# A two-layer trunk on one core: feed-forward blocks in pairs, with one sum per pair

## The chip, the core and the metric

The kernel runs on one core of a Trainium2 chip. The core has TensorE for matrix products, VectorE and ScalarE for element-wise work, GpSimd, and SyncE, whose queue (SP) starts nearly all transfers here. Each engine works through its own list of instructions in order, and semaphores tie the lists together. TensorE writes its sums into accumulator memory (PSUM), of which the kernel uses eight banks of 128 x 512 float32. The metric is the device time of the whole program in microseconds, as the median of several runs.

## The reference

Input is x of 1024 positions with 1024 channels. Two layers follow, each a token mixer and then a feed-forward part, with a layer norm after every part:

```python
for i in range(DEPTH):                      # DEPTH = 2
    mix = rwkv7_time_mix(h, ...) if i % 2 == 0 else s5_mix(h, ...)
    h = layer_norm(DN_ALPHA * h + mix, ln_g[2 * i], ln_b[2 * i])
    h = layer_norm(DN_ALPHA * h + sq_relu_mlp(h, mlp_w1[i], mlp_w2[i]), ...)

def sq_relu_mlp(x, w1, w2):                 # w1: 1024 x 4096, w2: 4096 x 1024
    return jnp.square(jax.nn.relu(x @ w1)) @ w2
```

The change lies in `sq_relu_mlp`. It is the largest part: two layers of two products of 1024 x 1024 x 4096.

## The kernel before

**Layout and halves.** Activations lie with channels on the 128 partitions and positions along the columns. The 1024 positions are worked in two halves of 512, called A (`hA`, its operand `xo`) and B (`hB`, `xoB`), each in eight tiles of 128 x 512.

**Three products for one.** Every float32 operand is split into a rounded high part and a low part: ScalarE casts (`S.copy`, L191), VectorE subtracts (L192). A product of two tiles is then three matmuls (`mm3`: high x high, high x low, low x high). A weight tile is loaded by SP into `wraw` (two buffers) and split into `whi` and `wlo` (three buffers each). It serves 12 matmuls of 512 columns.

**Blocks.** The 4096 inner channels are cut into 16 blocks of 256 (`KB2` = 2 tiles of 128). In `blocks`, `up(b)` makes two sums of 24 matmuls each, and for each of them Relu (L1126) and Square (L1127) on ScalarE and the split into the buffer `qbuf`. `down(b)` takes these two operands, makes eight sums of 6 matmuls, and VectorE adds each to the state (L1158; L1156 for the first block). `mlp` runs layer 0 so: `up(0)`, then for each b `up(b + 1)` and after it `down(b)`. The sums take banks in turn from `psd()`, three of them in layer 0, seven in the feed-forward of layer 1.

**Layer 1.** The first JB = 3 blocks run plainly for A, and later the same three for B. The other 13 run jointly for both halves (`both`): a scheme with seven products of half the inner length in place of eight, 84 matmuls up, and 96 down. It needs sums and differences of the halves, split into operands T1 to T4 (`tops`); T1 lies in the place of `qbuf`, T4 in the place of A's operand. For the plain blocks the low parts of the weights are made beforehand: while layer 0 works on B, `presplit` loads 24 weight tiles, splits them and stores the low parts in memory (`low`), and the plain blocks of layer 1 load these in place of the subtraction on VectorE (L224 is their cast).

**What sets the order.** A scheduler places the instructions on each engine by priority (the program's order, unless `rank` sets a base) in a model of the time. So the order on each engine is fixed when the program is built. Work such as the norm of one half is cut into steps that are woven in: each `weave(op, share)` lets `share` steps follow a VectorE operation of the feed-forward (`PACEU` for the splits of `up`, `PACED` for the adds of `down`).

**Around it.** In layer 0 the feed-forward of A runs partly beside the recurrence of half B. After 12 blocks (`INS1`) the projection `wo(1)` of half B is placed, and the norm of B is woven into the last blocks. Then the tables of the S5 mixer, the norm of A and the S5 scan of A run beside the feed-forward of B. `INS3` is the number of blocks of B after which the mixer's output is loaded (`yload`).

Of the kernel before, what the change touches and what calls it, by code (L numbers as in the profile page):

```python
# [22 lines left out]
INS1 = 12  # L23
INS2 = 13
VSH = (-1, 2, 2, 4, 64)
INS3 = 12
# [9 lines left out]
PRE = 6  # L36
PACEU = (2.0, 7.0)
PACED = (0.5, 1.3)
PREB = 3
JB = 3  # L40
# [39 lines left out]
def trunk(ctx, tc, A):  # L80
# [127 lines left out]
    def wload(src, kt, n, key=None, halved=False):  # L208
# [3 lines left out]
        for k0 in range(0, kt, step):  # L212
# [12 lines left out]
            else:  # L225
                split(raw, hi, lo, G if nw[0] % WLG[0] in WLG[1] and WLG[2] <= nw[0] < WLG[3] else V)
                if key and key[0] not in ("mw1", "mw2"):
# [5 lines left out]
    def presplit(tiles):  # L233

        for key, k0, src in tiles:
            raw = tp.tile([128, 512], F32, tag="la", name="pre", bufs=2)
            SP.dma_start(raw, src.rearrange("p k n -> p (k n)"))
            hi = tp.tile([128, 512], F32R, tag="m", name="prehi", bufs=2)
            S.copy(hi, raw)
            behind(V.tensor_sub(raw.bitcast(F32R), raw, hi.bitcast(F32)))  # L240
            low[key, k0] = dr.tile([128, 512], F32, name=f"low{len(low)}")
            SP.dma_start(low[key, k0], raw)
            for _ in range(PRE):
                yield 1
# [869 lines left out]
    def blocks(i, h, xo, qbuf):  # L1114
# [4 lines left out]
        def up(b):  # L1119
            qs[b] = []  # L1120
            pace_[0] = PACEU[i]
            for n in range(KB2):
                p = psd()
                dense(p, wload(A["mw1"][i, b * KB2 + n], KT, 128, ("mw1", i, b * KB2 + n)), xo)
# [8 lines left out]
        def kept(src, part):  # L1133
# [4 lines left out]
            SP.dma_start(lo.bitcast(F32).rearrange("p k n -> p (k n)"), part)  # L1138
            S.copy(hi, raw)
            return [(hi[:, k], lo[:, k]) for k in range(KB2)]  # L1140

        def down(b, first=False, cs=slice(0, HT), keep=None):
            for n2 in range(C // nw):
                if keep is None:
                    w = wload(A["mw2"][i, b, n2], KB2, nw, ("mw2", i, b, n2))
                else:
                    if (b, n2) not in keep:
                        keep[b, n2] = kept(A["mw2"][i, b, n2], low[("mw2", i, b, n2), 0])
                    w = keep[b, n2]
                for n in range(nw // 128):  # L1150
                    p = psd()[:, cs]
                    dense(p, [(x[:, n * 128 : (n + 1) * 128], y[:, n * 128 : (n + 1) * 128]) for x, y in w],
                          [(x[:, cs], y[:, cs]) for x, y in qs[b]])
                    z = h[n2 * (nw // 128) + n][:, cs]
                    if first:
                        weave(V.scalar_tensor_tensor(z, z, ALPHA, p, op0=ALU.mult, op1=ALU.add), PACED[i])  # L1156
                    else:
                        weave(V.tensor_add(z, z, p), PACED[i])  # L1158

        return up, down  # L1160

    def mlp(i, h, xo, qbuf):

        nb = 32 // KB2
# [439 lines left out]
    for n in range(INS3):  # L1604
        next(mb)
        if n == PREB:
            first_steps(presplit([((("mw1", 1, b * KB2 + n), k0, A["mw1"][1, b * KB2 + n][:, k0 : k0 + 4]))
                                  for b in range(JB) for n in range(KB2) for k0 in (0, 4)]
                                 + [((("mw2", 1, b, n2), 0, A["mw2"][1, b, n2])) for b in range(JB) for n2 in range(C * KB2 // 512)]), 99000)
    ys = yload(0)  # L1610
    run(mb)
    unweave()
# [31 lines left out]
    def second_half():  # L1644
        yield from norm_steps(hB, 2, 1, True, xoB)
        for k in range(4):
            a = t3[k]
            G.tensor_add(a, a, hB[k])
# [3 lines left out]
            tops[1].append(d)  # L1652

# [3 lines left out]
    for b in range(JB - 1):  # L1657
        ua(b + 1)
        da(b, b == 0)
# [112 lines left out]
```

## Time and profile before

| What | Value |
|---|---|
| median of 3 runs | 2596.31 us (2596.01 to 2599.6) |
| the profiled execution, its own time | 2585.47 us |
| its span, first to last instruction | 2583.5 us |
| mean granted clock of TensorE | 0.975 |
| busy: TensorE, VectorE, ScalarE, GpSimd | 95%, 69%, 47%, 16% |
| matmuls | 16684 |

In the trace a line number is that of the kernel's text, and that of a helper where the helper issues the instruction: L256 is every dense matmul, L191 and L192 are every split. Buffer numbers are left out, so `d` is any bank of a dense sum. Matmuls are pipelined, and each row's length overlaps the next one's; what one matmul costs is read from the distance between starts.

The stages, in us from the start: the recurrence with little beside it up to about 775; the recurrence of B beside the feed-forward of A up to 1040; the projection, the norm of B, the last blocks of A and the tables up to 1295; the S5 scan of A up to 1400; the feed-forward of B up to 1640; S5 of B and the gated outputs up to 1877; plain blocks of A up to 1950; joint blocks up to 2470; plain blocks of B, the last norm and the stores up to the end.

### The profile page before, as it was taken

Reading aid. Unit: us, or ns where it says so; the run is one execution under the profiler, and the core shown is the slowest. Engines: PE = TensorE matmul, PEld = TensorE weight load, DVE = VectorE, ACT = ScalarE, POOL = GpSimd, SP = SyncE. Lnnn points to the kernel's source line nnn. Section 1 sums busy time; section 2 is a strip of 40 time slices with the busy share of each in tenths; the row PEclk is TensorE's granted clock in tenths of the full one; section 3 lists DMA queues with packets and bytes.
Section 4 is the critical chain, followed back from the end, with each engine's and each line's share of the span. In section 5 each row is a group of like instructions: output and inputs, shape, how many; then the busy total and the mean of one; then the engine's idle time right before and its main releaser. Section 6 shows DMA issues by size and latency. Waiting matters only on the chain.

```text
span 2583.5 us, 43873 instructions
## 1 busy us (share of the span) xinstructions
PE 2466.0 (95%) x16684; PEld 2002.0 (77%) x16684; DVE 1794.0 (69%) x3443; ACT 1210.5 (47%) x2165; POOL 406.0 (16%) x336
## 2 busy tenths in 40 slices
PE   7989989989989999999999999999999999999997
PEld 5779767788767888777777878887887888888886
DVE  7477687577787776899886665676657555656555
ACT  7555575454454443345634444334565333343334
POOL 3110441331211102001000000100222111111111
PEclk9999989999899999999999999999999999999998
DMA  4765455664222324446565553244261111111233
GB/s 152 261 200 184 160 198 172 190 186 152 93 70 78 104 86 126 141 122 165 162 226 192 176 175 111 95 162 160 94 197 60 49 54 50 48 58 49 78 122 114
DMA packets 217682, 340.66 MB, mean 132 GB/s; under 512 B 21248, under 2 KB 81792, under 8 KB 217472
## 3 DMA queue, kind: packets, MB, share of 16 engines
q1 hardware_dynamic: 216320, 335.77, 40.9%
q8 instruction: 131, 2.15, 0.4%
q10 hardware_dynamic: 1152, 2.10, 0.2%
q14 instruction: 79, 0.65, 0.1%
HBM read 267.53 MB, written 70.25 MB: 131 GB/s over the span
## 4 chain that ended last, share of the span: by engine, by line
PE 69%; DVE 13%; DMA 9%; ACT 5%; issue 3%; SPq 1%; POOL 0%; ACTq 0%; DVEq 0%; POOLq 0%
PE d L256 51%; PE d L1195 10%; DVE wlo L192 2%; PE pA L672 1%; DMA wraw<-in_mw_dram 1%; ACT whi L191 1%; DMA yl<-s_y 1%; DVE hA L1158 1%; DMA pre<-in_mw_dram 1%; DMA ldsg<-s_sg 1%; DMA s_y<-yg 1%; PE pR L780 1%; DMA lda<-s_a 1%; DVE oAl L192 1%; PE pq L934 1%
## 5 line engine op out<-in xcount | busy, mean ns | idle before, releaser
L191 ACT CAST whi<-wraw 128x512 fp32r<-128x512 f32 x424 | 261.6, 619 | 487.1 <-PE d L256 249.8
L192 DVE TENSOR_TENSOR wlo<-wraw,whi 128x512 fp32r<-128x512 f32 x424 | 317.4, 750 | 201.1 <-ACT whi L191 197.2
L256 PE MATMUL d<-qbuf,whi 128*128 128x512 f32 x1152 | 365.2, 399 | 9.8 <-ACT rl L1126 4.7
L256 PE MATMUL d<-oAh,whi 128*128 128x512 f32 (+1 forms) x752 | 303.2, 409 | 13.1 <-ACT ev L493 5.5
L256 PE MATMUL d<-oAl,whi 128*128 128x512 f32 (+1 forms) x752 | 302.1, 403 | 7.7 <-DVE oAl L942 4.4
L256 PE MATMUL d<-oAh,wlo 128*128 128x512 f32 (+1 forms) x752 | 301.2, 404 | 3.5 <-DMA wlo<-low 1.9
L256 PEld LDWEIGHTS d<-qbuf,whi 128*128 128x128 f32 x1152 | 212.2, 189 | 63.1 <-DVE hA L1158 7.8
L256 PE MATMUL d<-qbuf,wlo 128*128 128x512 f32 x576 | 225.5, 394 | 0.0
L256 PE MATMUL d<-oBh,whi 128*128 128x512 f32 x496 | 195.9, 395 | 0.4 <-DVE hA L1158 0.4
L256 PE MATMUL d<-oBh,wlo 128*128 128x512 f32 x496 | 195.8, 395 | 0.0
L256 PE MATMUL d<-oBl,whi 128*128 128x512 f32 x496 | 193.7, 391 | 0.0
L256 PEld LDWEIGHTS d<-oAh,whi 128*128 128x128 f32 (+1 forms) x752 | 143.1, 192 | 48.0 <-ACT ev L493 7.8
L256 PEld LDWEIGHTS d<-oAl,whi 128*128 128x128 f32 (+1 forms) x752 | 144.4, 193 | 38.7 <-DVE oAl L942 4.8
L256 PEld LDWEIGHTS d<-oAh,wlo 128*128 128x128 f32 (+1 forms) x752 | 144.3, 193 | 36.2 <-DVE wlo L192 2.7
L256 PE MATMUL d<-ql,whi 128*128 128x512 f32 x416 | 163.1, 392 | 0.0
L256 PE MATMUL d<-qh,whi 128*128 128x512 f32 x416 | 162.0, 389 | 0.0
L256 PE MATMUL d<-qh,wlo 128*128 128x512 f32 x416 | 158.0, 394 | 0.0
L256 PEld LDWEIGHTS d<-qbuf,wlo 128*128 128x128 f32 x576 | 108.9, 189 | 24.4 <-issue 0.5
L1158 DVE TENSOR_TENSOR hA<-hA,d 128x512 f32<-128x512 f32 x136 | 92.0, 683 | 28.8 <-PE d L256 27.7
L1158 DVE TENSOR_TENSOR hB<-hB,d 128x512 f32<-128x512 f32 (+1 forms) x160 | 97.6, 631 | 20.1 <-PE d L256 18.9
L256 PEld LDWEIGHTS d<-oBh,wlo 128*128 128x128 f32 x496 | 93.2, 188 | 21.9 <-issue 0.8
L256 PEld LDWEIGHTS d<-oBh,whi 128*128 128x128 f32 x496 | 93.3, 188 | 21.5 <-issue 2.0
(495 smaller groups left out, 5268.6 us busy)
## 6 DMA issues: line engine op xcount, KB each, us to landing
wraw<-in_mw_dram SPq DMA_DIRECT2D x356, 256.0 KB, 2.7
wlo<-low SPq DMA_DIRECT2D x92, 256.0 KB, 2.9
wraw<-in_glu_dram SPq DMA_DIRECT2D x64, 256.0 KB, 2.7
low<-wlo SPq DMA_DIRECT2D x52, 256.0 KB, 2.6
raw<-in_mw_dram SPq DMA_DIRECT2D x52, 256.0 KB, 2.7
wraw<-in_wk_dram SPq DMA_DIRECT2D x32, 256.0 KB, 3.2
wraw<-in_wr_dram SPq DMA_DIRECT2D x32, 256.0 KB, 3.7
wraw<-in_wv_dram SPq DMA_DIRECT2D x32, 256.0 KB, 4.2
```

Of the source, the lines that this page charges most:

```text
L191: S.copy(hi, src)
L192: op = (e or V).tensor_sub(lo, src, hi.bitcast(F32))
L256: bulk.append((PE.matmul(p, w, x, **kw).ins, x.shape[-1]))
L672: prods.append(PE.matmul(pp[h][:, cc, i], D.KB[j][hs, u].rearrange("p j l -> p (j l)"), D.AR[j][hs, u].rearrange("p j l -> p (j l)"), star ...
L780: hop.append(PE.matmul(pR[hs, i], at[:, h, c, i, 0], vsa[:, cl, h, i], start=True, stop=True))
L934: PE.matmul(pq[:, j : j + 1], q[:, j * 128 : (j + 1) * 128], ones_c[:, 0:1], start=k + j == 0, stop=k == KT - 1, skip_group_check=True)
L1158: weave(V.tensor_add(z, z, p), PACED[i])
L1195: PE.matmul(p, w[:, k], x, start=not add and k + j == 0, stop=k == 3 and j == 2, skip_group_check=True)
```

## The change

`mlp` and the plain blocks of layer 1 now work in pairs: `up(b)`, `up(b + 1)`, then one `down((b, b + 1))`. This takes two banks at a time and adds the products of both blocks in them, 12 matmuls per bank, so that VectorE adds to the state once per pair. For each two banks the order is: both banks with block b, then both with block b + 1; in the first two banks block b + 1 is taken one operand at a time. `INS1` and `INS3` count pairs now (6 = 12 blocks).

In layer 1 there are JB = 4 plain blocks per half, two pairs, and 12 joint ones. `presplit` and the stored low parts of feed-forward weights are gone: VectorE splits these weights where they are used. `PACEU` is 2.0 in both layers (7.0 before in layer 1), `PACED` 0.5 (1.3 before in layer 1). The operand T4 is made step by step in `second_half` together with T2, from a copy, and no longer between the last plain up phase and the joint blocks.

```diff
-INS1 = 12
+INS1 = 6
-INS3 = 12
+INS3 = 6
-PACEU = (2.0, 7.0)
-PACED = (0.5, 1.3)
-JB = 3
+JB = 4
...
-        def down(b, first=False, cs=slice(0, HT), keep=None):
+        def down(bs, first=False, cs=slice(0, HT), keep=None):
...
+                nn = nw // 128
+                ps = [psd()[:, cs] for _ in range(nn)]
+                parts = [(w[k], qs[b][k]) for w, b in zip(ws, bs) for k in range(KB2)]
+                def products(n, js):
+                    for j in js:
+                        (x, y), (qh, ql) = parts[j]
+                        sl = slice(n * 128, (n + 1) * 128)
+                        mm3(ps[n], x[:, sl], y[:, sl], qh[:, cs], ql[:, cs], j == 0, j == len(parts) - 1)
+                last = len(parts) - 1
+                groups = [range(KB2 * m, KB2 * m + KB2) for m in range(len(bs))]
+                if n2 == 0 and len(bs) > 1:
+                    groups[-1:] = [(j,) for j in groups[-1]]
+                turns_ = [(n, js) for js in groups for n in range(nn)]
...
-        up(0)
-        for b in range(nb):
-            if b + 1 < nb:
-                up(b + 1)
-            down(b, b == 0)
+        for b in range(0, 32 // KB2, 2):
+            up(b)
+            up(b + 1)
+            down((b, b + 1), b == 0)
             yield
...
-    for b in range(JB - 1):
-        ua(b + 1)
-        da(b, b == 0)
+    ua(1)
+    da((0, 1), True)
+    ua(2)
+    ua(3)
     unweave()
...
-    for b in range(JB - TB):
-        ub(b + 1)
-        db(b)
-    for b in range(JB - TB + 1, JB):
-        ub(b)
+    ub(1)
+    db((0, 1))
+    ub(2)
+    ub(3)
```

**TensorE, a down phase of half B in layer 0.** `d_16863` is the last sum of an up phase, `qbuf` the operands of the down phase, `whi` and `wlo` its weights. Before:

```order
L256 MATMUL d_16863<-oBh_12551,wlo_16873 128x512
L256 MATMUL d_16911<-qbuf_9633,whi_16907 128x512 x2
L256 MATMUL d_16911<-qbuf_9633,wlo_16908 128x512
...
L256 MATMUL d_16919<-qbuf_9633,whi_16907 128x512 x2
...
L256 MATMUL d_16933<-qbuf_9633,whi_16929 128x512 x2
L256 MATMUL d_16933<-qbuf_9633,wlo_16930 128x512
```

After the change, with `d_16471` as the last sum of the pair's up phases, `whi_16515` as block b's weights and `whi_16521` as those of block b + 1:

```order
L239 MATMUL d_16471<-oBh_12399,wlo_16481 128x512
L239 MATMUL d_16525<-qbuf_9633,whi_16515 128x512 x2
...
L239 MATMUL d_16526<-qbuf_9633,whi_16515 128x512 x2
...
L239 MATMUL d_16525<-qbuf_9633,whi_16521 128x512 x2
L239 MATMUL d_16525<-qbuf_9633,wlo_16522 128x512
L239 MATMUL d_16526<-qbuf_9633,whi_16521 128x512 x2
L239 MATMUL d_16526<-qbuf_9633,wlo_16522 128x512
L239 MATMUL d_16565<-qbuf_9633,whi_16555 128x512 x2
...
L239 MATMUL d_16525<-qbuf_9633,whi_16521 128x512
L239 MATMUL d_16526<-qbuf_9633,whi_16521 128x512
```

Before, each bank is closed after 6 matmuls, and the block that the up phase has just made is not read. Now two banks stay open, and the operand of the last up phase is first read in the last two rows: after 6 + 6 matmuls with block b, 3 + 3 with the first operand of block b + 1, and 6 of the next bank, which the scheduler has pulled forward.

**VectorE, the start of the joint blocks in layer 1.** `raw` and `s2` are the first joint weights, `oAl` is a part of T4, `t2` of T2, `t1r` goes into T1, the adds to `hA` are those of the last plain blocks. Before:

```order
L1158 TENSOR_TENSOR hA_7722<-hA_7722,d_20432 128x512
L192 TENSOR_TENSOR t2_20267<-t3r_19672,t2_20266 128x512
L1670 TENSOR_TENSOR t3r_19632<-t3r_19632,hB_12067 128x512
L192 TENSOR_TENSOR wlo_20484<-raw_20470,whi_20483 128x512
L1158 TENSOR_TENSOR hA_7762<-hA_7762,d_20440 128x512
L192 TENSOR_TENSOR t2_20280<-t3r_19686,t2_20279 128x512
L192 TENSOR_TENSOR wlo_20503<-s2_20479,whi_20502 128x512
L1158 TENSOR_TENSOR hA_7802<-hA_7802,d_20454 128x512
L192 TENSOR_TENSOR oAl_20364<-t3r_19618,oAh_20363 128x512
L1158 TENSOR_TENSOR hA_7842<-hA_7842,d_20462 128x512
L192 TENSOR_TENSOR wlo_20520<-raw_20472,whi_20519 128x512
L192 TENSOR_TENSOR qbuf_20349<-t1r_19616,qbuf_20349 128x512
```

After the change:

```order
L188 TENSOR_TENSOR oAl_20014<-tb_19977,oAh_20013 128x512
L1157 TENSOR_TENSOR hA_7682<-hA_7682,d_20083 128x512
L188 TENSOR_TENSOR wlo_20153<-wraw_20150,whi_20152 128x512
L188 TENSOR_TENSOR wlo_20159<-wraw_20156,whi_20158 128x512
L1157 TENSOR_TENSOR hA_7722<-hA_7722,d_20122 128x512
L1157 TENSOR_TENSOR hA_7762<-hA_7762,d_20123 128x512
L188 TENSOR_TENSOR wlo_20204<-raw_20190,whi_20203 128x512
L188 TENSOR_TENSOR wlo_20223<-s2_20199,whi_20222 128x512
L1157 TENSOR_TENSOR hA_7802<-hA_7802,d_20162 128x512
L1157 TENSOR_TENSOR hA_7842<-hA_7842,d_20163 128x512
L188 TENSOR_TENSOR wlo_20240<-raw_20192,whi_20239 128x512
L188 TENSOR_TENSOR qbuf_20017<-t1r_19184,qbuf_20017 128x512
```

T2 and T4 now stand before this place, the first among the weights of the plain blocks, and the splits of those weights (`wraw`) have come in.

**SP, the feed-forward of half B in layer 0.** `wraw` are weights of the running blocks, `pre` and `low` the loads and stores of `presplit`. Before:

```order
L242 DMA low64_15918<-pre_15913 128x512
L215 DMA wraw_16022<-in_mw1_dram 128x512
L237 DMA pre_16028<-in_mw2_dram 128x512
L215 DMA wraw_16065<-in_mw1_dram 128x512
L242 DMA low65_15991<-pre_15986 128x512
L215 DMA wraw_16071<-in_mw1_dram 128x512
L242 DMA low66_16033<-pre_16028 128x512
L237 DMA pre_16077<-in_mw2_dram 128x512
```

After the change:

```order
L211 DMA wraw_16263<-in_mw2_dram 128x512
L211 DMA wraw_16346<-in_mw1_dram 128x512
L211 DMA wraw_16352<-in_mw1_dram 128x512
L211 DMA wraw_16388<-in_mw1_dram 128x512
L211 DMA wraw_16394<-in_mw1_dram 128x512
```

The queue holds weight loads alone there.

More of the change, by code (lines that the diff above doesn't have):

```diff
@@ L226, in wload @@
                 split(raw, hi, lo, G if nw[0] % WLG[0] in WLG[1] and WLG[2] <= nw[0] < WLG[3] else V)
-                if key and key[0] not in ("mw1", "mw2"):
+                if key:
                     low[key, k0] = dr.tile([128, 512], F32, name=f"low{len(low)}")
@@ L231, in wload @@
         return out
[L233 to L244, printed above, removed]
     def inorder(prods):
@@ L1137, in kept @@
                       for t in ("t1", "t2"))
-            SP.dma_start(lo.bitcast(F32).rearrange("p k n -> p (k n)"), part)
-            S.copy(hi, raw)
+            split(raw, hi, lo)
             return [(hi[:, k], lo[:, k]) for k in range(KB2)]
-        def down(b, first=False, cs=slice(0, HT), keep=None):
+        def down(bs, first=False, cs=slice(0, HT), keep=None):
             for n2 in range(C // nw):
[L1144 to L1154, printed above, removed]
+                ws = []
+                for b in bs:
+                    if keep is None:
+                        ws.append(wload(A["mw2"][i, b, n2], KB2, nw))
+                    else:
+                        if (b, n2) not in keep:
+                            keep[b, n2] = kept(A["mw2"][i, b, n2])
+                        ws.append(keep[b, n2])
+                nn = nw // 128
[11 more added lines that the diff above has]
+                turns_ = [(n, js) for js in groups for n in range(nn)]
+                for n, js in turns_:
+                    products(n, js)
+                    if last not in js:
+                        continue
+                    z, p = h[n2 * nn + n][:, cs], ps[n]
@@ L1603, in trunk @@
     mb = mlp(0, hB, xoB, qbuf)
-    for n in range(INS3):
+    for _ in range(INS3):
         next(mb)
[L1606 to L1609, printed above, removed]
     ys = yload(0)
     run(mb)
-    unweave()
     with rank(99000):
@@ L1652, in second_half @@
             tops[1].append(d)
+            behind(V.tensor_sub(a, a, hB[k + 4]))
+            yield 1
+            tops[3].append(operand(a))
+            yield 1
     ua, da = blocks(1, hA, xo, qbuf)
@@ L1668, in trunk @@
             tops[0].append(d)
-        for k in range(4):
-            V.tensor_sub(t3[k], t3[k], hB[k + 4])
-            tops[3].append(operand(t3[k]))
-    da(JB - 1, JB == 1)
+    da((2, 3))
     uj, dj = both(1, hB, hA, xoB, xo, tops, JB)
@@ L1684, in trunk @@
     store(0, hA)
-    for b in range(JB - TB):
-        ub(b + 1)
-        db(b)
-    for b in range(JB - TB + 1, JB):
-        ub(b)
+    ub(1)
+    db((0, 1))
+    ub(2)
+    ub(3)
     keep = {}
     for c in range(2):
-        for b in range(JB - TB, JB):
-            db(b, False, slice(256 * c, 256 * c + 256), keep)
+        db(tuple(range(JB - TB, JB)), False, slice(256 * c, 256 * c + 256), keep)
         if c == 0:
```

17 lines of the change are left out of this document (7 added, 10 removed).

## The prediction, made before the changed kernel had run

> **What bounds the kernel now.** I read the page first: the share of each engine, the granted clock and the chain of work that ended last.
>
> ```profile
> PE 2466.0 (95%) x16684; PEld 2002.0 (77%) x16684; DVE 1794.0 (69%) x3443; ACT 1210.5 (47%) x2165; POOL 406.0 (16%) x336
> PEclk9999989999899999999999999999999999999998
> PE 69%; DVE 13%; DMA 9%; ACT 5%; issue 3%; SPq 1%; POOL 0%; ACTq 0%; DVEq 0%; POOLq 0%
> ```
>
> TensorE is busy 95% of 2583.5 us and carries 69% of the chain. So the question is how many matmuls there are, and where TensorE waits. The chain in order of time gives the price of one matmul. These are two neighbouring joint blocks, the same piece of each (start, length, engine, line, count):
>
> ```profile
> 2074.18 20.16 PE d L256 x88
> 2115.38 20.16 PE d L256 x88
> ```
>
> 88 matmuls of 512 columns take 20.16 us, so **229 ns each**. The starts are 41.20 us apart, which is 180 x 229 ns: a joint block (84 matmuls up, 96 down) runs with no wait at all.
>
> Next I cut the span into its stages and asked for each engine's busy time there (window: length, then TensorE, weight loads, VectorE, ScalarE, GpSimd; clock; DMA share; GB/s). The blocks that change start just before 775 us.
>
> ```profile
> 775.00:1040.00 265.00, 263.43 (x1976) 210.98 (x1974) 191.56 (x398) 112.37 (x203) 33.92 (x28) 1.00 0.34 104
> 1040.00:1060.00 20.00, 19.07 (x80) 14.82 (x81) 18.36 (x65) 11.53 (x22) 0.00 (x0) 1.00 0.59 182
> 1060.00:1295.00 235.00, 227.73 (x1247) 176.62 (x1247) 211.53 (x381) 116.21 (x212) 21.85 (x15) 0.99 0.50 143
> 1295.00:1400.00 105.00, 100.84 (x1167) 81.72 (x1163) 78.65 (x171) 40.99 (x75) 0.00 (x0) 1.00 0.61 210
> 1400.00:1560.00 160.00, 156.75 (x681) 126.94 (x680) 99.03 (x157) 74.58 (x128) 0.00 (x0) 1.00 0.55 177
> 1560.00:1640.00 80.00, 80.00 (x352) 65.82 (x351) 47.19 (x72) 29.95 (x50) 2.47 (x2) 1.00 0.33 98
> 1877.00:1950.00 73.00, 68.65 (x305) 55.77 (x303) 45.74 (x67) 45.24 (x78) 20.77 (x14) 1.00 0.53 170
> 1950.00:2470.00 520.00, 519.66 (x2263) 426.19 (x2264) 304.09 (x449) 191.14 (x325) 85.59 (x62) 1.00 0.19 58
> 2470.00:2540.00 70.00, 67.79 (x321) 56.16 (x320) 40.49 (x65) 31.32 (x54) 8.10 (x6) 1.00 0.43 142
> ```
>
> TensorE's idle time (length less busy time) is small everywhere: 2.5 us in the first two rows, **7.3** in 1060:1295, then 4.2, 3.3, 0, 4.4, 0.3 and 2.2. In 1060:1295 VectorE is busy 211.53 of 235 us (90%): the tail of the first feed-forward, the norm of half B and the S5 tables all stand on it. Nothing before 775 us is touched.
>
> Who ends these waits, from the waits of TensorE asked stage by stage (sum, times, longest). The first two rows are of 775:1060, the next two of 1060:1295, then one of 1400:1640, one of 1877:1955, one of 2470:2545:
>
> ```profile
> PE d L256 <- DVE hA L1158: 0.9, 2, 0.5
> PE d L256 <- DVE hA L1156: 0.7, 1, 0.7
> ...
> PE d L256 <- DVE hA L1158: 3.0, 3, 1.8
> PE pb L1443 <- DVE bp L1416: 1.4, 1, 1.4
> ...
> PE d L256 <- ACT rl L1126: 3.0, 3, 1.6
> ...
> PE d L1195 <- DVE wlo L192: 4.1, 1, 4.1
> ...
> PE d L256 <- ACT rl L1126: 2.2, 1, 2.2
> ```
>
> A down product waits for a bank that VectorE has not added yet (0.9, 0.7 and 3.0 us) or that ScalarE has not squared (3.0 and 2.2 us); the first joint block waits 4.1 us for its split weights.
>
> **Matmuls.** JB goes from 3 to 4: one joint block (180) becomes two plain blocks (2 x 96 = 192). That is 12 x 229 ns = **+2.7 us**. All other matmuls are the same ones in another order.
>
> **Adds.** A pair adds once per bank. Counted in the two orders of instructions, 152 adds of 512 columns and 16 of 256 fall away, and 52 + 8 weight splits come; what one costs:
>
> ```profile
> L1158 DVE TENSOR_TENSOR hA<-hA,d 128x512 f32<-128x512 f32 x136 | 92.0, 683 | 28.8 <-PE d L256 27.7
> L192 DVE TENSOR_TENSOR wlo<-wraw,whi 128x512 fp32r<-128x512 f32 x424 | 317.4, 750 | 201.1 <-ACT whi L191 197.2
> ```
>
> 152 x 0.68 = 104 us of VectorE work go and 60 x 0.75 = 45 us come, nearly all of that in layer 1. None of it is worth anything while TensorE does not wait. In 1060:1295 it does. There VectorE loses some 23 adds (16 us). The waits named for it, 3.0 + 1.4 us, should go, and a little of the 2.9 us that no quoted row names: I take **-5**, with bounds 0 (the table chain itself is late) and -7.3 (all idle time of the row). In 775:1060, 1.6 of 2.5 us are waits for such adds, half of them at the first block, which stays: **-1**, bounds 0 and -2.5. In 1295:1400 the S5 outputs set the waits: **-1**, bounds 0 and -4.2.
>
> **Presplit.** 24 loads, 24 casts, 24 subtractions and 24 stores leave the B feed-forward of layer 0, and 48 loads of stored low parts leave layer 1. What they cost is seen at 1492 us, on SP's queue, ScalarE and TensorE:
>
> ```profile
> 1484.46 0.33 SPq L242 DMA_DIRECT2D low<-pre  x1
> 1486.49 0.33 SPq L237 DMA_DIRECT2D pre<-in_mw_dram  x1
> 1486.91 6.01 SPq L215 DMA_DIRECT2D wraw<-in_mw_dram  x3
> ...
> 1491.23 0.62 ACT L191 CAST whi<-wraw 128x512 fp32r<-128x512 f32 x1 [1.53 <-DMA wraw<-in_mw_dram]
> 1491.75 0.59 ACT L1126 ACTIVATE rl<-d 128x512 f32<-128x512 f32 x1
> ...
> 1492.39 0.73 PE L256 MATMUL d<-qbuf,whi 128*128 128x512 f32 x2 [1.64 <-ACT rl L1126]
> ```
>
> SP issues in order: the weight loads stand behind the store and the presplit's load, the cast waits 1.53 us for its weights, the Relu stands behind the cast, and TensorE waits 1.64 us for the Relu's bank. Of the 3.0 us in this stage one wait (about 1 us) belongs to the load of y, which stays. So **-2**, bounds 0 and -3.3.
>
> **Joint start.** The 4.1 us arise because VectorE does the sums and splits for T2 and T4 just ahead of the first joint weights; with the change these are woven into the plain blocks, and the first joint splits stand ahead of the rest of them. **-4.1**, bounds 0 and -4.4. **Last blocks.** The 2.2 us are a Relu behind stores and casts on ScalarE; the stores now stand a whole block earlier: **-1.5**, bounds 0 and -2.2.
>
> **The new wait.** Until now down(b) came after up(b+1), so its operands were 11 us old. Now the pair's last operand comes from the up phase just before. In a quiet place that takes (last up matmul, first down matmul, Relu, subtraction):
>
> ```profile
> 1600.67 0.39 PE L256 MATMUL d<-oBh,wlo 128*128 128x512 f32 x1
> 1600.90 0.63 PE L256 MATMUL d<-qbuf,whi 128*128 128x512 f32 x2
> ...
> 1601.39 0.59 ACT L1126 ACTIVATE rl<-d 128x512 f32<-128x512 f32 x1
> ...
> 1603.34 0.69 DVE L192 TENSOR_TENSOR qbuf<-rl,qbuf 128x512 fp32r<-128x512 f32 x1 [0.16 <-ACT qbuf L191]
> ```
>
> The operand is whole at 1604.03, 3.1 us after the up phase ended at 1600.90. In the new order 24 matmuls (5.5 us) stand between in such a place, 18 (4.1 us) by the code alone. So 1.0 to 2.4 us are to spare, and the wait costs nothing. Beside a norm it is otherwise. The same two steps at 1278 us:
>
> ```profile
> 1278.36 0.39 PE L256 MATMUL d<-oBh,wlo 128*128 128x512 f32 x1
> ...
> 1282.77 0.59 ACT L1126 ACTIVATE rl<-d 128x512 f32<-128x512 f32 x1
> ...
> 1287.11 0.69 DVE L192 TENSOR_TENSOR qbuf<-rl,qbuf 128x512 fp32r<-128x512 f32 x1
> ```
>
> Here the operand is whole at 1287.80, 9.2 us after the up phase ended at 1278.59: 3.7 us too late. Behind the waiting matmul stands all of TensorE. Seven pairs lie beside a norm or the load of y: A's last two, B's first two and B's seventh in layer 0, and one of each half in layer 1. With nothing late this costs 0, with all seven so late 26 us. VectorE has less to do there now, so I take **+3**.
>
> **Splits beside GpSimd.** In 1877:1950 GpSimd runs 14 instructions. There VectorE's instructions with two operands in SBUF are stretched, as the groups of that window show:
>
> ```profile
> L192 DVE TENSOR_TENSOR oBl<-hB,oBh 128x512 fp32r<-128x512 f32 x5 | 4.8, 985 | 0.0
> L1665 DVE TENSOR_TENSOR t1r<-t1r,hB 128x512 f32<-128x512 f32 x4 | 4.3, 1068 | 0.0
> L192 DVE TENSOR_TENSOR qbuf<-rl,qbuf 128x512 fp32r<-128x512 f32 x6 | 4.2, 692 | 15.6 <-ACT qbuf L191 15.6
> ```
>
> Undisturbed ones take 692, the stretched ones around 1030 ns in the mean, singly up to 1.78 us. Now 32 splits come here in four blocks instead of three: VectorE's 45.7 us of 73 become about 45.7 + 32 x 0.69 - 8 x 0.68 + 10 x 0.69 (T4 and two more operands) = 69 us of 88 us (384 x 229 ns). That fits on average, but the weights are split only two or three tiles ahead. Bounds: 0, and 14 stretched by 1.1 us each = 15; I take **+1.5**, since the mean load is 78%.
>
> [...]
>
> **Sum:** 2.7 - 5 - 1 - 1 - 2 - 4.1 - 1.5 + 3 + 1.5 = **-7.4 us**. The profiled execution took 2585.47 us by its own time (span 2583.5, 2 us around it), so it would be about 2578. The median of the runs shown is 2596.31, 10.8 us above the profiled one; the same difference on it gives **2589 us**.
>
> **Rivals.**
> *The new wait takes the gain back.* If the seven pairs are late by half of what 1278 us shows (13 instead of 3 us), the sum is +2.6: 2599. For it: ScalarE and VectorE put norm work ahead of feed-forward work. Against it: 16 us less VectorE work in just that stretch.
> *The adds were no limit.* If the waits in 775:1400 come from the table and S5 chains, the 7 us there stay: sum -0.4, 2596. For it: the row on pb waits for a table step. Against it: 3.0 us wait for adds by name.
> *Slower: the plain blocks of layer 1 become bound by VectorE.* One mechanism: 32 new splits beside 14 GpSimd instructions. If each stretches a split, the stage costs 15 instead of 1.5 us: sum +6.5, 2603. It decides once VectorE's 69 + 15 us meet the stage's 88 us in bunches, that is once splits come later than the 5.5 us that two tiles ahead give. Against it: the stretched instructions of before ended in one 4.1 us wait only.
> *Larger gain.* If all idle time of the stages from 775 to 1560 and of 1877 on goes (about 24 us) and nothing new comes, the sum is -21: 2575.
>
> **Chances.** Forecast (2583 to 2594) 0.40, first two rivals together 0.27, slower 0.13, larger gain 0.20. The range that leaves out 2 in 10 reaches from 2576 to 2604; the forecast's own is 2583 to 2594. A measurement of this kernel tells 0.2% (5.2 us) from no change: faster means under 2591.1. The forecast lies under it in about 0.8 of its range and the larger gain wholly: 0.32 + 0.20 = 0.52. Of the first two rivals 0.03 lie above 2601.5: slower 0.16, same 0.32.
>
> **What would show it.** In the new profile: the waits "d <- DVE hA" in the S5-table stretch near zero; no 1 to 2 us wait for the Relu in B's feed-forward except at the load of y; no 4 us wait at the first joint block; joint blocks still 41.2 us apart, twelve of them. A wait of a down product for the subtraction of the pair's last operand, or for split weights in layer 1's plain blocks, of more than 5 us in sum would prove my +3 or +1.5 wrong. If idle time falls and the time does not, matmuls stand further apart than 229 ns, and the whole sum was made against the wrong quantity.

## The result, and the profile after

| | before | after the change |
|---|---|---|
| median of the first comparison (6 runs each) | 2596.11 us | 2579.47 us (2572.82 to 2584.3) |
| ratio, 95% interval | | **0.9946** (0.9926 to 0.9966) |
| second comparison (31 and 12 runs) | 2587.82 us | 2576.08 us, 0.9959 (0.9940 to 0.9978) |
| the profiled execution, its own time | 2585.47 us | 2581.69 us |
| its span | 2583.5 us | 2580.0 us |

The change is faster by about 0.5%, 10 to 14 us. The forecast was 2589 us. The time, 2579.5 us, lies inside the wide range (2576 to 2604), but below the forecast's own (2583 to 2594) and nearer to the rival of a larger gain (2575). The two profiled executions differ by 3.5 us only. A part of the missing rest lies ahead of the change: the same program, in the same order, reached the product `pU<-vsa,kbt` just ahead of the first down phase at 757.28 us in the profile before and at 765.61 after, 8.3 us later. So the table of stretches below counts from a product shortly ahead of that place; a window that is given in us from the start is off by such amounts between two profiles.

The page of the changed kernel: each engine's busy time, the granted clock, and the chain that ended last by engine.

```profile
PE 2471.4 (96%) x16696; PEld 2009.5 (78%) x16696; DVE 1720.1 (67%) x3300; ACT 1202.2 (47%) x2144; POOL 405.4 (16%) x331
PEclk9999989899989999999999999999999999999998
PE 73%; DVE 10%; DMA 9%; ACT 4%; issue 2%; SPq 1%; POOL 0%; ACTq 0%; DVEq 0%; POOLq 0%
```

There are 12 more matmuls, 143 fewer instructions on VectorE, and TensorE carries 73% of the chain in place of 69%. Two neighbouring joint blocks in its chain (start, length):

```profile
2093.74 20.16 PE d L239 x88
2134.94 20.16 PE d L239 x88
```

They are 41.20 us apart, as before. (L239 is now the line of the dense matmuls, L187 and L188 are cast and subtraction of a split, L1157 the add.) The stages of the changed kernel, columns as before:

```profile
775.00:1040.00 265.00, 265.00 (x2017) 212.93 (x2016) 169.09 (x367) 112.97 (x203) 35.86 (x28) 1.00 0.33 97
1060.00:1295.00 235.00, 229.73 (x1173) 177.36 (x1173) 205.57 (x381) 114.67 (x207) 26.44 (x15) 0.99 0.46 130
1877.00:1950.00 73.00, 72.86 (x325) 59.76 (x324) 52.64 (x76) 42.55 (x74) 14.09 (x10) 1.00 0.31 96
2470.00:2540.00 70.00, 68.87 (x328) 57.28 (x328) 44.28 (x70) 36.22 (x60) 5.16 (x4) 1.00 0.37 117
```

TensorE's idle time fell from 1.6 to 0 us in the first row, from 7.3 to 5.3 in the second, from 4.4 to 0.1 in the third and from 2.2 to 1.1 in the last. What ends the waits now (the first row of 775:1060, three of 1060:1295, two of 1400:1640, then one each of 1877:1955 and 2470:2545):

```profile
PE d L239 <- DVE hA L1157: 0.6, 1, 0.6
...
PE d L239 <- DVE wlo L188: 3.8, 1, 3.8
PE pk L1424 <- DVE ca L1413: 0.8, 1, 0.8
PE d L239 <- ACT whi L187: 0.5, 1, 0.5
...
PE py L1527 <- DMA tt<-tT: 2.2, 1, 2.2
PE d L239 <- ACT whi L187: 1.0, 1, 1.0
...
PE d L239 <- DVE qbuf L188: 1.0, 1, 1.0
...
PE d L239 <- ACT kt L187: 1.1, 1, 1.1
```

The waits for `hA` in the table stretch are gone, as are the Relu waits and the 4.1 us at the first joint block. New is a single wait of 3.8 us for a weight split in the table stretch. A wait of the S5 scan for a load (`tt`) is 2.2 us long; before it was 1.2 us, at a place ahead of 1400 us.

**Where the time went.** In every kernel below but one (the second read of each bank), TensorE's dense products, that is all matmuls that write a bank `d`, 512 or 256 columns wide, can be counted from the start. The table gives the time from one product to another, in us, from the starts of these instructions in each profile. Up to product 2200 all kernels are the same program (it lies 10.8 us ahead of the piece `pU<-vsa,kbt` named in the expectations, so those figures are the last column less 10.8). 2200 to 3200 is A's feed-forward beside the recurrence of B, 3200 to 5200 the rest of layer 0, 5200 to 6400 S5 of B and the gated outputs, 6400 to 6600 the end of A's plain blocks and the first joint block. The last stretch holds the 12 extra matmuls where there are four plain blocks.

```
                2200-3200 3200-5200 5200-6400 6400-6600 6600-end  2200-end   ratio to before, 95%
before              291.3     560.8     332.5      52.8    599.6    1837.0
the change          287.4     556.2     335.5      47.5    598.5    1825.1   0.9946 (0.9926 to 0.9966)
the change again    289.1     556.4     331.4      47.6    596.7    1821.2   0.9959 (0.9940 to 0.9978)
no presplit         291.4     552.6     332.5      58.0    601.1    1835.7   1.0027 (1.0014 to 1.0040)
before, four plain  291.4     571.1     333.6      45.5    598.4    1839.9   0.9985 (0.9971 to 0.9999)
pairs in layer 0    287.4     564.8     329.8      53.4    596.0    1831.4   0.9995 (0.9981 to 1.0009)
layer 0 single      290.9     557.2     330.5      47.5    596.8    1823.0   0.9961 (0.9944 to 0.9979)
first pair only     287.3     562.8     331.1      47.5    596.5    1825.3   0.9973 (0.9955 to 0.9992)
no turns            287.3     559.4     332.3      47.5    596.5    1823.1   0.9952 (0.9933 to 0.9971)
layer 1 single      287.3     558.1     333.3      55.2    596.5    1830.4   0.9981 (0.9963 to 0.9999)
T4 late             288.8     556.9     334.0      53.3    598.0    1830.9   0.9981 (0.9966 to 0.9997)
three plain         288.8     560.4     332.7      63.1    599.1    1844.1   1.0023 (1.0007 to 1.0039)
slower weave        288.5     549.8     333.4      47.5    600.3    1819.5   0.9922 (0.9899 to 0.9946)
```

Before against the mean of the two profiles of the change: -3.1, -4.5, +1.0, -5.3, -2.0, together -13.9 us.

These stretches hold more than waits. TensorE's rows behind the 3.8 us wait of the changed kernel (start, length):

```profile
1130.17 0.80 PE L239 MATMUL d<-oAh,wlo 128*128 128x512 f32 x1 [3.85 <-DVE wlo L188]
1130.76 0.63 PE L239 MATMUL d<-oAh,whi 128*128 128x512 f32 x1
1131.19 0.63 PE L239 MATMUL d<-oAl,whi 128*128 128x512 f32 x1
...
1135.81 0.39 PE L239 MATMUL d<-oAh,whi 128*128 128x512 f32 x1
1136.04 0.39 PE L239 MATMUL d<-oAl,whi 128*128 128x512 f32 x1
```

Behind the first one the matmuls start 427 ns apart, from 1135.81 us on 230 ns: the 13 from 1130.17 to 1135.81 take 5.6 us in place of 3.0, and the granted clock from 1128.9 to 1135.7 us is 0.50. So 2.7 us are lost at this wait beyond its own length, and no idle time shows them. How often this happens is told in the last section.

### The profile page after: what moved, and what is told of

It reads as the page before. It is cut to its first block, busy times and chain, and to the rows that moved or that the text cites. A ratio compares the mean times of both kernels' runs of the same rounds, so it can differ in the third digit from the quotient of the medians.

```text
span 2580.0 us, 43512 instructions
## 1 busy us (share of the span) xinstructions
PE 2471.4 (96%) x16696; PEld 2009.5 (78%) x16696; DVE 1720.1 (67%) x3300; ACT 1202.2 (47%) x2144; POOL 405.4 (16%) x331
## 4 chain that ended last, share of the span: by engine, by line
PE 73%; DVE 10%; DMA 9%; ACT 4%; issue 2%; SPq 1%; POOL 0%; ACTq 0%; DVEq 0%; POOLq 0%
PE d L239 54%; PE d L1192 9%; DMA wraw<-in_mw_dram 2%; DVE wlo L188 1%; DMA ldsg<-s_sg 1%; PE pA L655 1%; DMA yl<-s_y 1%; ACT whi L187 1%; DMA s_y<-yg 1%; PE pk L1424 1%; DMA s_r<-ev 1%; DMA wraw<-in_wr_dram 1%; PE pR L763 1%; DVE oAl L188 1%; PE pU L773 1%
## 5 line engine op out<-in xcount | busy, mean ns | idle before, releaser
L187 ACT CAST whi<-wraw 128x512 fp32r<-128x512 f32 x476 | 294.9, 620 | 592.7 <-PE d L239 329.8
L188 DVE TENSOR_TENSOR wlo<-wraw,whi 128x512 fp32r<-128x512 f32 x476 | 353.4, 744 | 269.6 <-ACT whi L187 258.9
L239 PE MATMUL d<-qbuf,whi 128*128 128x512 f32 x1216 | 376.0, 395 | 1.7 <-DVE qbuf L188 1.0
L239 PE MATMUL d<-oAh,whi 128*128 128x512 f32 (+1 forms) x768 | 310.2, 410 | 14.7 <-ACT ev L476 7.2
L239 PE MATMUL d<-oAl,whi 128*128 128x512 f32 (+1 forms) x768 | 310.7, 406 | 8.4 <-DVE oAl L925 4.4
L239 PE MATMUL d<-oAh,wlo 128*128 128x512 f32 (+1 forms) x768 | 309.8, 406 | 8.0 <-DVE wlo L188 5.8
L239 PEld LDWEIGHTS d<-qbuf,whi 128*128 128x128 f32 x1216 | 225.7, 188 | 51.0 <-DVE qbuf L188 1.4
L239 PE MATMUL d<-qbuf,wlo 128*128 128x512 f32 x608 | 233.2, 395 | 0.0
L239 PE MATMUL d<-oBh,wlo 128*128 128x512 f32 x512 | 202.0, 396 | 1.3 <-DVE wlo L217 1.2
L239 PE MATMUL d<-oBh,whi 128*128 128x512 f32 x512 | 202.1, 395 | 1.0 <-ACT whi L187 1.0
L239 PE MATMUL d<-oBl,whi 128*128 128x512 f32 x512 | 200.9, 392 | 0.0
L239 PEld LDWEIGHTS d<-oAh,whi 128*128 128x128 f32 (+1 forms) x768 | 147.1, 193 | 51.1 <-ACT ev L476 9.5
L239 PEld LDWEIGHTS d<-oAh,wlo 128*128 128x128 f32 (+1 forms) x768 | 148.4, 194 | 41.7 <-DVE wlo L188 7.5
L239 PEld LDWEIGHTS d<-oAl,whi 128*128 128x128 f32 (+1 forms) x768 | 148.1, 193 | 40.3 <-DVE oAl L188 5.1
L239 PE MATMUL d<-ql,whi 128*128 128x512 f32 x384 | 150.7, 392 | 0.0
L239 PE MATMUL d<-qh,whi 128*128 128x512 f32 x384 | 147.9, 390 | 0.0
L239 PE MATMUL d<-qh,wlo 128*128 128x512 f32 x384 | 145.9, 394 | 0.0
L239 PEld LDWEIGHTS d<-qbuf,wlo 128*128 128x128 f32 x608 | 114.2, 188 | 26.3 <-DVE wlo L188 0.9
L239 PEld LDWEIGHTS d<-oBh,wlo 128*128 128x128 f32 x512 | 96.3, 188 | 25.1 <-DVE wlo L217 1.6
L239 PEld LDWEIGHTS d<-oBh,whi 128*128 128x128 f32 x512 | 96.5, 189 | 21.6 <-ACT whi L187 1.4
L239 PEld LDWEIGHTS d<-oBl,whi 128*128 128x128 f32 x512 | 96.3, 188 | 21.1 <-issue 0.6
L1251 DVE TENSOR_TENSOR hA<-hA,d 128x512 f32<-128x512 f32 x96 | 66.0, 687 | 40.7 <-PE d L239 40.6
```

The lines of the kernel that those rows point to most:

```text
L187: S.copy(hi, src)
L188: op = (e or V).tensor_sub(lo, src, hi.bitcast(F32))
L239: bulk.append((PE.matmul(p, w, x, **kw).ins, x.shape[-1]))
```

## The experiments

**The change again.** 

> The changed kernel itself, again and beside the others. Both theories expect 0.994 to 0.996 of the kernel before, and 1814 us from the piece pU<-vsa,kbt to the end, as in its first profile; how far a second profile of the same program lies from the first says what a difference of two profiles is worth (expected: under 2 us in that stretch, against some 10 us in the whole span).

The second profile is 3.9 us shorter behind product 2200, twice what was expected, and 4.1 us of it lie between 5200 and 6400. The window of that stretch in the first profile:

```profile
1740.00:1877.00 137.00, 132.36 (x855) 108.03 (x855) 91.44 (x139) 61.11 (x107) 18.89 (x13) 0.96 0.39 130
```

and in the second:

```profile
1740.00:1877.00 137.00, 132.26 (x872) 107.59 (x871) 91.84 (x135) 61.00 (x106) 18.88 (x13) 1.00 0.37 125
```

TensorE is busy the same time, at a granted clock of 0.96 and of 1.00, and gets 17 matmuls more done at the higher one. So differences of 4 us between two single profiles say nothing in a stretch with such a dip; in 2200 to 3200 profiles of the same order differ by up to 1.7 us, and between 6400 and 6600, for all kernels with the change's layer 1, by 0.1 us.

**The presplit alone taken out.**

```diff
-PACEU = (2.0, 7.0)
-PACED = (0.5, 1.3)
+PACEU = (2.0, 2.0)
+PACED = (0.5, 0.5)
...
-        if n == PREB:
-            first_steps(presplit([...]), 99000)
-                dense(p, wload(A["mw1"][...], KT, 128, ("mw1", i, b * KB2 + n)), xo)
+                dense(p, wload(A["mw1"][...], KT, 128), xo)
```

> The kernel before, with the presplit alone taken out: no load, cast, subtraction and store of layer 1's low parts in B's feed-forward, and VectorE splits layer 1's weights as everywhere else; blocks stay single, three plain blocks stay. The measure is the stretch from the recurrence's piece of products pU<-vsa,kbt at 757.28 us (before) to the end of the span: 2583.5 - 757.28 = 1826.2 us before, 2580.0 - 765.61 = 1814.4 us after the change; what lies ahead of it is the same program. Theory (presplit cost 2 us of TensorE's time, the splits in layer 1 are hidden): 1824, and the waits for the Relu near 1492 us go. Rival (the presplit was hidden, and split weights in the plain blocks beside GpSimd are what it saved): 1828 to 1841, with waits for wlo in the first three blocks of layer 1.

The weave in layer 1 got the change's density along with it. Both held, each at its own place. In B's feed-forward of layer 0 TensorE is never idle any more. The window 1420 to 1640 us of the kernel before:

```profile
1420.00:1640.00 220.00, 216.97 (x946) 176.83 (x945) 134.14 (x209) 96.59 (x163) 2.47 (x2) 1.00 0.47 147
```

and without presplit:

```profile
1420.00:1640.00 220.00, 220.00 (x965) 180.86 (x964) 123.92 (x187) 83.45 (x139) 3.00 (x2) 1.00 0.31 96
```

19 more matmuls in the same 220 us, 19 x 229 ns = 4.3 us: that was the presplit's price. But at the first joint block 5.2 us come. The waits of TensorE from 1900 to 1975 us in this kernel:

```profile
PE d L256 <- DVE hA L1157: 3.0, 2, 1.5
PE d L256 <- DVE wlo L192: 2.8, 3, 1.5
PE d L1194 <- ACT whi L191: 1.3, 2, 1.1
PE d L256 <- ACT whi L191: 1.2, 1, 1.2
```

Sums and splits meet on VectorE; that the denser weave has no part in these 5.2 us was not tried. In all it is 0.27% slower than before: without the rest of the change, taking the presplit out loses. The one profile does not show where, since from product 2200 on it is 1.3 us shorter than the one of before.

**Pairs in layer 0 alone, and all but these.** The first gives the kernel before the new `down` and `mlp`; the second gives the changed kernel the old order:

```diff
-        for b in range(0, 32 // KB2, 2):
-            up(b)
-            up(b + 1)
-            down((b, b + 1), b == 0)
+        up(0)
+        for b in range(32 // KB2):
+            if b + 1 < 32 // KB2:
+                up(b + 1)
+            down((b,), b == 0)
```

> The kernel before, with pairs in both feed-forwards of layer 0 and nothing else: the presplit stays, layer 1 stays in three single plain blocks. Theory (the halved adds relieve VectorE where TensorE waited for it): 7 us less than the kernel before, 1819 us in the stretch from the piece pU<-vsa,kbt at 757 us to the end, most of it between 1060 and 1295 us. Rival (the adds were no limit, and the change gained by the presplit and by layer 1 alone): 1825 to 1827.

> The changed kernel with the feed-forwards of layer 0 as single blocks again, one up ahead of each down as before; no presplit, layer 1 in pairs. Theory (the pairs of layer 0 are worth 7 us): 1821 us in the stretch from the piece pU<-vsa,kbt to the end, against 1814.4 of the changed kernel, the waits d <- DVE hA back between 1060 and 1295 us. Rival (worth nothing): 1814. If the parts of the change don't add up (this run and the run with pairs in layer 0 alone give different prices for the same pairs), the presplit and the pairs stood in each other's way.

By the runs the rivals were nearer. Pairs in layer 0 alone do not change the time (0.9995, interval around 1), and the changed kernel without them (0.9961) is not told apart from the change. (The profile of the first, 1820.6 us from the piece on, falls on the theory's side, but it is of an execution 11 us under that kernel's median.) The 5 us expected between 1060 and 1295 us are not there: 3200 to 5200 costs 4.0 us more with pairs beside the presplit, and without it the change (556.2 and 556.4) lies between the two profiles of single blocks (552.6 and 557.2). What the pairs gain lies earlier, 2 to 4 us in 2200 to 3200. The wait that goes there stands between 757 and 785 us in "layer 0 single" (and, with 1.8 us, in the kernel before), not in the change:

```profile
PE pb L631 <- POOL kf L626: 1.9, 1, 1.9
```

**The first pair only.** The changed kernel with single blocks in layer 0 except A's first two.

```diff
-        for b in range(0, 32 // KB2, 2):
-            up(b)
-            up(b + 1)
-            down((b, b + 1), b == 0)
+        up(0)
+        up(1)
+        if pair:
+            down((0, 1), True)
+            yield
+            up(2)
+        else:
+            down((0,), True)
...
-    ma = mlp(0, hA, xo, qbuf)
+    ma = mlp(0, hA, xo, qbuf, True)
```

> The changed kernel with single blocks in layer 0 again, except the first pair of A, which lies beside the end of half B's recurrence. Theory after the runs so far (of the pairs in layer 0 only this one counts, because its down phase, and with it eight sums on VectorE, starts a whole up phase later and falls behind the recurrence's steps): the stretch between the piece pU<-vsa,kbt and the 2400th full-width product is as short as in the changed kernel, 5 us shorter than with single blocks throughout, and the whole is within 2 us of the changed kernel. Rival (the pairs gain over the whole of layer 0): no more than 1 of these 5 us.

2200 to 3200 takes 287.3 us, as short as in any kernel and 3.6 to 4.1 us shorter than with single blocks, and the wait for `kf` is gone. Of this the wait itself is 1.9 us; in "layer 0 single" 6.8 us at half the clock begin 1.4 us behind it, and this profile has none there. The place of the gain is shown: a down phase twice as long stands ahead of the small product `pb`, and GpSimd's `kf` is ready when TensorE comes to it. Eight more sums come later too; that these matter is not shown. The whole stretch from 2200 on is within 0.2 us of the change's first profile.

**VectorE's load put back.** A second read of each bank, as a sum over its row:

```diff
+                    if i == 0:
+                        V.tensor_reduce(spent, p, axis=AX.X, op=ALU.add)
```

> The changed kernel, and behind each added bank of layer 0's feed-forwards VectorE reads the same bank once more (a sum over its row into one unused column): its load and the time that it holds a bank are those of single blocks again, while the order of TensorE's work stays that of pairs. The output is not touched. Theory (pairs gain by VectorE's load): about 1819 to 1821 us in the stretch from the piece pU<-vsa,kbt to the end, waits for hA or for weights between 1060 and 1295 us. Rival (pairs gain by the order of the products, by work that is spread otherwise): 1814 to 1815.

It took 2687.22 us (ratio 1.0390), and says nothing on the load. The instructions of its tile, what VectorE waited for ahead of them:

```profile
L1161 DVE TENSOR_REDUCE spent<-d x128: 671/681/692, 909.6 to 1739.3; 128x1 f32<-128x512 f32 x128
  DMA s_y<-gt: 2.4, 1
```

The first read stands at 909.6 us, behind a store of the recurrence of B (`s_y<-gt`), and every later sum stands behind it. The likely reason is that the one column was given memory that the recurrence still used; it was not tried with another place.

**No turns by operand.**

```diff
-                if n2 == 0 and len(bs) > 1:
-                    groups[-1:] = [(j,) for j in groups[-1]]
```

> The changed kernel without the order that takes the pair's last block one operand at a time in the first quarter of the down phase: there the last operand is wanted after 18 products in place of the last 12 of 48. Theory (the wait for the last operand is real where VectorE or ScalarE has norm work, and the order by operands hides most of it): 2 to 8 us slower than the changed kernel, new waits d <- DVE qbuf. Rival (no operand is late with either order): equal within 1 us, no wait for qbuf.

The rival held: 1823.1 us lies between the two profiles of the change, 0.9952 between their ratios. The one wait for `qbuf` in A's plain blocks stays at 1.0 us with either order.

**Layer 1 in single blocks; T4 late; three plain blocks.** Three edits of the changed kernel, one each:

```diff
-    da((0, 1), True)
+    da((0,), True)
     ua(2)
+    da((1,))
     ua(3)
+    da((2,))
...
-    da((2, 3))
+    da((3,))
...
-    db((0, 1))
+    db((0,))
     ub(2)
+    db((1,))
```
```diff
-            behind(V.tensor_sub(a, a, hB[k + 4]))
-            yield 1
-            tops[3].append(operand(a))
-            yield 1
...
+        for k in range(4):
+            V.tensor_sub(t3[k], t3[k], hB[k + 4])
+            tops[3].append(operand(t3[k]))
     da((2, 3))
```
```diff
-JB = 4
+JB = 3
...
-    ua(3)
...
-    da((2, 3))
+    da((2,))
...
-    db((0, 1))
+    db((0,))
     ub(2)
-    ub(3)
```

> The changed kernel with layer 1's four plain blocks single in A, and the first two single in B (its last pair stays); T4 is still woven in early and VectorE splits the weights. Theory (the run without the presplit lost 5.2 us at the first joint block because splits and a sum per block and bank meet on VectorE; the pairs of layer 1 are what pays for the splits): 3 to 6 us slower than the changed kernel, waits for wlo and hA between 1900 and 1950 us. Rival (T4's early place alone removes the wait, pairs in layer 1 are worth nothing): equal within 1 us.

> The changed kernel with the operands of T4 made where they were before: by VectorE in one piece ahead of the last plain down phase, not woven into the plain blocks; pairs, four plain blocks and VectorE's splits stay. Theory of the prediction (T4's early place is what removes the 4.1 us wait at the first joint block): about 4 us slower than the changed kernel, a wait for wlo of some 4 us there. Theory after the runs so far (the cover that four paired blocks give removes it, since three plain blocks cost 15.6 us at that place and single ones 7.3 us): equal within 2 us.

> The changed kernel with three plain blocks of layer 1 in each half, a pair and a single one, so one more joint block and 12 matmuls of 229 ns fewer. Theory (the fourth plain block costs its matmuls, 2.7 us, and nothing hangs on it): 2.7 us faster than the changed kernel, 1811.5 us in the stretch from the piece pU<-vsa,kbt to the end. Rival (the fourth block is needed as cover for the splits and for the norm of B beside it): 1814 to 1820, with waits between 1877 us and the first joint blocks.

Each of the three edits brings waits back at the same place: 7.7 us (55.2 against 47.5), 5.8 us and 15.6 us. TensorE's waits from 1900 to 1975 us with layer 1 single:

```profile
PE d L239 <- DVE wlo L188: 6.4, 2, 6.0
```

with T4 late:

```profile
PE d L239 <- DVE wlo L188: 5.2, 3, 3.9
```

and with three plain blocks:

```profile
PE d L1192 <- ACT whi L187: 4.6, 1, 4.6
PE d L239 <- DVE wlo L188: 3.6, 1, 3.6
PE d L239 <- ACT qbuf L187: 2.7, 2, 2.1
```

The prices are above the waits, of which the change has 1.0 us itself: 5.4 us of waits more for 7.7, 4.2 for 5.8 and 9.9 for 15.6. The rest is within what the half clock costs here: 6.8, 3.4 and 13.7 us of these stretches run at 0.50, which by the starts of the matmuls (427 ns apart in place of 227) is worth half of that at most.

My expectation for T4, formed after the first runs, fell: cover alone does not do it, and the prediction's own term for T4 (-4.1) was nearer. How late VectorE gets is seen in the kernel with layer 1 single. Instructions of GpSimd in order of time, and behind the dots those of VectorE:

```profile
1917.76 2.60 POOL L1640 TENSOR_TENSOR tb<-t3r,hB 128x512 f32<-128x512 f32 x2 [6.52 <-ACT hB L1003]
1921.37 1.30 POOL L188 TENSOR_TENSOR oBl<-hB,oBh 128x512 fp32r<-128x512 f32 x1 [1.01 <-ACT oBh L187]
1924.87 1.31 POOL L188 TENSOR_TENSOR oBl<-hB,oBh 128x512 fp32r<-128x512 f32 x1 [2.20 <-ACT oBh L187]
...
1919.08 1.82 DVE L188 TENSOR_TENSOR qbuf<-rl,qbuf 128x512 fp32r<-128x512 f32 x1
...
1923.22 0.68 DVE L1664 TENSOR_TENSOR t1r<-t1r,hB 128x512 f32<-128x512 f32 x1
1925.02 1.70 DVE L1664 TENSOR_TENSOR t1r<-t1r,hB 128x512 f32<-128x512 f32 x1
```

The two of these VectorE instructions that start while GpSimd works take 1.82 and 1.70 us, the one in GpSimd's pause 0.68; all have two operands in SBUF. Two more `t1r` from 1927.84 us on take 2.36 us together, and there the view shows no instruction of GpSimd. What stretches them is not shown, nor how much of the 6.4 us of waits comes from it.

**The kernel before with four plain blocks.**

```diff
-JB = 3
+JB = 4
```

> The kernel before with four plain blocks of layer 1 in place of three: single blocks, presplit (now of four blocks), nothing else. Theory (a fourth plain block is cover by itself, for the norm of B and the sums of T2 and T4): 4.1 us of wait go at the first joint block and 2.7 us of matmuls come, 1 to 2 us faster than the kernel before, 1825 us from the piece pU<-vsa,kbt to the end. Rival (cover was no need where the weights are split ahead, the wait stays): 2.7 us slower, 1829 us.

The wait at the first joint block goes wholly (45.5 us; 200 x 229 ns is 45.8). But the eight tiles more of presplit cost the gain again. TensorE's waits from 1420 to 1640 us:

```profile
PE d L256 <- ACT rl L1126: 5.0, 4, 2.3
PE d L256 <- DVE hB L1158: 2.9, 3, 2.0
```

They sum to 7.9 us, where the kernel before had 3.0. The stretch from the piece to the end, 1829.1 us, is the rival's, but not by its mechanism. Its time is 0.15% below before, at the edge of what can be told.

**A slower weave.**

```diff
-            pace_[0] = 2.0
+            pace_[0] = 1.0 if i == 0 else 2.0
```

> The changed kernel with the norm's steps woven behind the splits of layer 0's up phases at half the density: one step for each split in place of two. In the changed kernel seven subtractions hB<-hB,pm stand in one row of 4.27 us on VectorE ahead of a weight split, and TensorE waits 4.0 to 4.4 us for that split near 1130 us. Theory (the row of norm steps is the cause): the row falls to three at a time, the wait to under 2 us, 2 to 3 us faster in the stretch from the piece pU<-vsa,kbt to the end: 1808 to 1812 us against 1810.4 and 1814.4 in two profiles of the changed kernel. Rival (VectorE is simply full there with the S5 tables, the wait moves to another instruction): equal within 1 us.

VectorE's row of the norm in the change, in order of time (start, length):

```profile
1122.37 4.27 DVE L976 TENSOR_TENSOR hB<-hB,pm 128x512 f32<-128x512 f32 x7
```

and its pieces in this kernel:

```profile
1119.06 1.27 DVE L976 TENSOR_TENSOR hB<-hB,pm 128x512 f32<-128x512 f32 x2
1126.07 1.87 DVE L976 TENSOR_TENSOR hB<-hB,pm 128x512 f32<-128x512 f32 x3
1129.54 1.88 DVE L976 TENSOR_TENSOR hB<-hB,pm 128x512 f32<-128x512 f32 x3
```

The wait for `wlo` is gone between 1060 and 1200 us; a wait of 2.0 us for another step of the norm (`pr <- rb`) stands there now. 3200 to 5200 takes 549.8 us against 556.2 and 556.4, more than the 2 to 3 us expected. The clock explains most of it: in this stretch both profiles of the change have 10.2 us at half the clock, 6.8 of them at the wait for `wlo` and 3.4 at the scan's wait for `tt`, worth 5.1 us at most; this profile has none. The S5 scan also stands elsewhere in the order; what that is worth was not separated. The time is 2569.1 us, 0.9922 of before (0.9899 to 0.9946). That is the fastest kernel of this study; against the change it was not timed side by side, and its interval overlaps those of the change (0.9926 to 0.9966 and 0.9940 to 0.9978). So that it is faster than the change is likely, not shown.

## Why the prediction was right, and where it was wrong

The sign was right. The sum was -7.4 us; the two profiles show -11.9 and -15.8, the two ratios -14 and -11. That the time still fell into the range is in part luck: the adds were priced too high, but the presplit too low, and of the 4.5 us for new waits and stretched splits 1.0 came. One thing stands at nothing in the whole sum: I priced every wait by its idle time alone, and the half clock at many of them (427 ns from one matmul to the next in place of 227) is in no term.

- **Matmuls, +2.7:** right as a count and a price (x16696, 41.20 us). Wrong as a view of JB: I treated the fourth plain block as a cost alone. With three plain blocks the change is slower than the kernel before (1.0023), since the cover for VectorE's splits is gone.
- **Adds, -5, -1, -1: the step that failed, though the forecast held.** The waits for `hA` went, as foreseen, but I took idle time named for an add as time that the add's removal gives back. In 1060 to 1295 us the idle time fell by 2.0 only: seven norm subtractions in one row, 4.27 us on VectorE, and five steps of the tables behind them held up a weight split instead. The half clock behind that wait cost 2.7 us more, against at most 1.7 us (3.41 us at 0.50) behind a wait for `hA` in the kernel before. Over layer 0 pairs are worth nothing that can be measured (0.9995 beside the presplit).
- **"Nothing before 775 us is touched": wrong.** The first down phase starts at 760.9 us. That pair gives 2 to 4 us, by a wait for GpSimd that I had not looked at (1.8 us in the kernel before), and by the clock behind it (3.41 us at 0.50 there).
- **Presplit, -2: mis-sized.** The mechanism was right, the term is 4.3 us. I left one of the three named Relu waits standing for the load of y; without presplit it went too (idle 0.00), and the count of matmuls in the stage tells more than the waits named.
- **Joint start, -4.1, and splits beside GpSimd, +1.5:** measured together -5.3. It adds up: the wait of 4.1 us went and one of 0.6 us for `hA`, eight matmuls behind the former, which had taken 3.5 us at half the clock in place of 1.8, run at full pace, and 1.0 us for the pair's last operand came, 5.4 us in all. T4's early place is worth 5.8 by itself. No split of the plain blocks is late by more than 0.3 us.
- **Last blocks, -1.5:** the Relu wait of 2.2 us went, one of 1.1 us for `kt` came. From 6600 to the end the change took 2.0 us less although it has 2.7 us more matmuls there; single profiles spread by about as much.
- **The new wait, +3:** 1.0 us at one place, and the order by operands makes no difference. VectorE and ScalarE were early enough beside the norms.
- **The slower rival:** single instructions beside GpSimd are stretched, as it said, but the change did not pay for it: from 1877 to 1950 us its four `t1r` took 1208 ns in the mean and five `oBl` 852, the 24 splits `wlo<-wraw` 752, against 690 of the six `qbuf`. That each of GpSimd's instructions holds up a split, as in the upper bound of 15 us, no run shows. That three plain blocks cost its price (15.6 against 15 us) is a coincidence: 9.9 us of it are waits and the rest goes with the half clock, and no run shows that the stretched splits make these waits. What decides is how many plain blocks there are, whether their sums are halved and when T4 is made; the change has all three, and I weighed only T4's place.

So the gain is no sum of independent parts. Taking the presplit out gives 4.3 us and costs 5.2; single blocks, T4 late or three blocks each cost 6 to 16. The parts of layer 1 pay for each other.

## What to carry to other kernels

A wait named for one instruction of a busy engine isn't that instruction's price: when it goes, the next one in that engine's row can be late (here a wait of 3.8 us for a weight split came in place of 3.0 us for adds), so look at what stands behind it before counting the idle time as gained. And look at the matmuls behind a wait: if they start further apart than elsewhere (here 427 ns against 227), more is lost there than the wait's length. Work that is moved onto an engine can need cover beside it (without the fourth plain block the change took 15.6 us more at that place), and an extra piece of plain work (here 2.7 us) can be the cheapest cover. Where runs scatter, compare profiles by counting the same instruction in both, from the last place where the programs are equal.

## What the runs showed of the hardware that was not expected

Each trace keeps the granted clock with the time of every change. In the thirteen profiles of the table it has two values, 1.00 and 0.50. The stretches at 0.50 between 750 and 2520 us last 3.41, 6.83 or 10.24 us: one, two or three times the same length. A dense matmul of 512 columns starts 427 ns behind the one before in them, and 227 ns outside (both the median; the mean over a joint block is 229).

There are 45 such stretches in all, and 41 of them begin during a wait of TensorE of at least 1.5 us or in the 5 us behind it; the other four lie near 775 us among the small products of the recurrence. All 16 idle stretches of TensorE there of 3.4 us or more have one in them or up to 3.5 us behind them, and so do 24 of the 49 of 1.5 to 3.4 us. So a stretch at 0.50 comes with some short waits and not with others, and a program's executions differ by that: from 1740 to 1877 us the change has a granted clock of 0.96 in one profile and 1.00 in the other. "No presplit" and "layer 0 single" give TensorE the same 13715 matmuls in the same order, up to 1901 us. Both wait for the same load of the S5 scan (`tt`), 3.0 us from 1364.6 us on and 2.8 us from 1365.6 us on; a row of the stages of the former:

```profile
1340.00:1420.00 80.00, 74.68 (x643) 60.57 (x636) 54.82 (x101) 34.37 (x61) 0.00 (x0) 1.00 0.61 205
```

and of the latter:

```profile
1340.00:1420.00 80.00, 75.11 (x652) 60.89 (x645) 54.53 (x104) 32.06 (x57) 0.00 (x0) 0.94 0.60 201
```

At 0.94 the 200 dense products from 4200 on, among S5's small ones, took 72.7 us against 69.1. The latter has one stretch of 10.24 us at 0.50, from 1366.6 us on, and the former none in this window; 10.24 of the 80 us at 0.50 and the rest at 1.00 make the 0.94. What brings the clock down, and what decides whether a wait of 2 or 3 us has a stretch at half clock, is not shown.
